# FFN up-projections: products of 512 columns into four banks, or of 256 columns into two

## The chip, the cores and the metric

The kernel runs on one core of a Trainium2 chip. The metric is device microseconds for one execution. TensorE is named PE in the profile, its weight loads PEld, VectorE DVE, ScalarE ACT, GpSimd POOL and SyncE SP.

## The reference

Two decoder layers over 256 positions of width 2048, all in float32. Layer 0 mixes with forgetting attention (16 heads of 128), layer 1 with sliding-window attention (32 query heads, 4 key heads of 64). After each mixer comes a gated ConvFFN. Every sub-layer is wrapped in a shift, a scale and a gate that come from a conditioning vector, and in a LayerNorm. The part that matters here:

```
def conv_ffn(h, w_up, conv_w, conv_b, w_down):          # D_FF = 5632, CONV_WIDTH = 3
    u = h @ w_up                                        # (256 x 2048) @ (2048 x 11264)
    up = jnp.pad(u, ((0, 0), (CONV_WIDTH - 1, 0), (0, 0)))
    u = sum(up[:, j:j + S] * conv_w[j] for j in range(CONV_WIDTH)) + conv_b
    g, val = u[..., :D_FF], u[..., D_FF:]
    return (jax.nn.silu(g) * val) @ w_down

x = layer_norm(DEEPNORM_ALPHA * x + (1.0 + gate) * F(x * (1.0 + scale) + shift), ln_g, ln_b)
```

## The kernel before

Every large product is made of three products in the float32r form. A weight tile `w` (two chunks of 128 rows by 512 columns, 512 KB, one DMA on SP's queue) is rounded by ACT into `wh` (L276), and DVE subtracts to get the remainder `wl` (L287). The activations are kept in the same way: `hHL[:, kc, 0, :]` is the rounded part `hH` of chunk kc (128 features by 256 positions), `hHL[:, kc, 1, :]`, right behind it in memory, the remainder `hL`. A product then adds `wh*hH + wh*hL + wl*hH`. A "tile" below is one such weight tile with all its products.

Three ways to use a tile stand side by side:

- `x_mm` (L298): activations are the stationary operand, weights move past in products of 512 columns. Their results are called `xs`. The down-projections of the FFN (`xs<-wh,gT`, `xs<-wl,gT`), both output projections and all of layer 1's input projections use it.
- `w_mm` (L325): weights are stationary, 128 columns at a time, and the activations move past in products of 256 columns: for each of the 8 cells (2 chunks, 4 column groups f) one product with `hH` and one with `hL`, both for the same weights, and then 8 products of `wl` with `hH`. Results are called `ws`, two banks of PSUM for the 4 column groups. Layer 0's query and key projections use it.
- the inner `use` of `w_stationary` (L344): the same, but `hH` and `hL` move past in one product of 512 columns, so that a bank holds `wh*hH` plus `wl*hH` in its left half and `wh*hL` in its right half. Results are called `wd`, four banks for the 4 column groups. The up-projections use it.

Each FFN has 22 column blocks of 512 for its two halves, gate and value, in two passes: 6 pairs of blocks (96 tiles) and the down-projection of what they give, then 5 pairs (80 tiles) and the rest of the down-projection. That is 352 tiles of up-projection in the two layers, and 176 of down-projection. When a block is done, a generator (`evac`, L1073) is put into a list and makes one step at each later tile: ACT copies the right half of a bank (L1060), DVE adds the left half to it (`summed`, L1061), ACT scales it by one tap of the convolution and adds the bias (L1066), DVE adds the other two taps (L1067, L1069), and then follows the SiLU (gate half) or the product with it and the split into `gT` (value half, L1089, L85, L86).

Beside this, the conditioning vectors of later sub-layers are computed on DVE (`acc`, L406) at a rate of so many steps a tile, and are finished on PE by small products (`sm<-acc,ones` and `sm<-ones,acc`). At the start of an FFN the activations come in over the first tiles: PE transposes the normalised x (`sm<-ident,x`), ACT and DVE turn that into `hHL`. `feed()` issues one such step within a tile.

Instructions are written in the order above and a scheduler then orders them by its own rules for each engine, except where `pin` holds them in program order. The semaphore waits follow from the tiles.

Of the kernel before, what the change touches and what calls it, by code (L numbers as in the profile page):

```python
# [10 lines left out]
F32 = mybir.dt.float32  # L11
F32R = mybir.dt.float32r
I32 = mybir.dt.int32
AF = mybir.ActivationFunctionType
ALU = mybir.AluOpType
AX = mybir.AxisListType

P = 128
D = 2048
S = 256  # L20
NT = S // P
KC = D // P
# [8 lines left out]
CW = 3  # L31
# [10 lines left out]
def hybrid_trunk(ctx: ExitStack, tc: tile.TileContext, a: dict, out: bass.AP):  # L42
    nc = tc.nc
# [9 lines left out]
    tp = ctx.enter_context(tc.tile_pool(name="tp", bufs=4))  # L53
# [3 lines left out]
    def wtile(name="w"):  # L57
        return wp.tile([P, 2, WB], F32, tag="w", name=name)

    def gtile(name="g"):  # L60
        return gp.tile([P, 2, S], F32R, tag="g", name=name)

    def ttile(name="t"):
        return tp.tile([P, 2 * S], F32, tag="t", name=name)

    def bank(name="sm"):
        return psp.tile([P, 512], F32, tag="ps", name=name)

    def w_banks():
        return [bank("ws").rearrange("p (a s) -> p a s", a=2) for _ in range(2)]  # L70
# [4 lines left out]
    def mm(o, lhsT, rhs, start=False, stop=False, **kw):  # L75
        return nc.tensor.matmul(o, lhsT, rhs, start=start, stop=stop, **kw)  # L76

    def pin(ins, on=True):

        if on:  # L80
            tc.keep_in_program_order(ins)

    def split(h, l, src):

        nc.scalar.copy(h, src)  # L85
        nc.vector.tensor_tensor(l, src, f32(h), op=ALU.subtract)  # L86
# [123 lines left out]
    def then(fn):  # L210

        work.append(fn)
        if len(work) == 1 and not ahead[0]:
            settle()
# [3 lines left out]
    def settle(left=0):  # L218
        while work and (ahead[0] > left or not left):
            f = work.pop(0)  # L220
            rest(f, *work)
            f()
# [24 lines left out]
    def defer(gen):  # L247

        post.append(gen)

    def run_post():
        for g in list(post):
            if next(g, post) is post:
                post.remove(g)
# [7 lines left out]
    def feed():  # L262

        if feeds and not fed[0]:
            fed[0] = True
            feeds.pop(0)()

    def stream(wsrc, row0, col, ks, use):

        for kc in ks[::2]:  # L270
            r0 = (row0 + kc) * P
            w = wtile()
            pin(nc.sync.dma_start(w, wsrc[r0:r0 + 2 * P, col:col + WB].rearrange("(k p) f -> p k f", p=P)), False)
            h = hl.tile([P, 2, WB], F32R, tag="wh", name="wh")
            l = hl.tile([P, 2, WB], F32R, tag="wl", name="wl")
            pin(nc.scalar.copy(h, w), False)  # L276

            def go(kc=kc, h=h, l=l):
                ahead[0] -= 1
                run_post()  # L280
                fed[0] = False
                use(kc, h, l)
                feed()
                tick()

            def residual_(w=w, h=h, l=l, go=go):
                pin(nc.vector.tensor_tensor(l, w, f32(h), op=ALU.subtract), go in behind)  # L287
                del residuals[go]

            if any(f in stops for f in work) and sum(f in behind for f in work) < 2:  # L290
                behind.add(go)
            ahead[0] += 1
            weights.add(go)
            residuals[go] = residual_
            work.append(go)
            settle(2)
# [28 lines left out]
    def w_mm(ps, kc, h, l, last=KC - 1, first=0):  # L325

        cells = [(i, f, ps[f // 2][:, f % 2, :]) for i in range(2) for f in range(4)]
        for i, f, o in cells:
            wh = h[:, i, f * P:(f + 1) * P]
            mm(o, wh, hH[:, kc + i, :], start=kc + i == first and f % 2 == 0, skip_group_check=True)  # L330
            mm(o, wh, hL[:, kc + i, :], skip_group_check=True)
        for i, f, o in cells:
            mm(o, l[:, i, f * P:(f + 1) * P], hH[:, kc + i, :], stop=kc + i == last, skip_group_check=True)

# [6 lines left out]

    def w_stationary(wsrc, col):

        ps = [bank("wd") for _ in range(4)]  # L344

        def use(kc, h, l):
            cells = [(i, f) for i in range(2) for f in range(4)]
            for i, f in cells:
                mm(ps[f], h[:, i, f * P:(f + 1) * P], hHL[:, kc + i].rearrange("p a s -> p (a s)"),
                   start=kc + i == 0)  # L350
            feed()
            for i, f in cells:
                mm(ps[f][:, :S], l[:, i, f * P:(f + 1) * P], hH[:, kc + i, :], stop=kc + i == KC - 1)

        stream(wsrc, 0, col, list(range(KC)), use)
        return ps


# [18 lines left out]
    def drain():  # L377
        while bg["wait"] or bg["run"]:
            step()

    def tick():
        ada_tick()
        if not feeds:
            step()
# [64 lines left out]
    def ada_need(l, v):  # L449
        n = 0  # L450
        while (l, v) not in cols and (l, v) not in gates:
            ada_step()
            n += 1
        if n:
            print("caught up", l, v, n)


    hHL = cst.tile([P, KC, 2, S], F32R, name="hHL")
    hH, hL = hHL[:, :, 0, :], hHL[:, :, 1, :]
# [593 lines left out]
    def conv_ffn(l):  # L1053
        w_up, w_dn = a["ffn_w_up"][l], a["ffn_w_down"][l]
        NB = DFF // WB
        cw = lambda j, f: ccol[:, l, j, f:f + 1]

        def summed(pf):
            s = tp.tile([P, S], F32, tag="s", bufs=2, name="s")
            nc.scalar.copy(s, pf[:, S:])  # L1060
            nc.vector.tensor_tensor(s, pf[:, :S], s, op=ALU.add)  # L1061
            return s

        def conv(s, f):
            u = tp.tile([P, S], F32, tag="u", bufs=2, name="u")
            nc.scalar.activation(u, s, AF.Identity, bias=cw(CW, f), scale=cw(2, f))  # L1066
            nc.vector.scalar_tensor_tensor(u[:, 1:], s[:, :S - 1], cw(1, f), u[:, 1:],  # L1067
                                           op0=ALU.mult, op1=ALU.add)
            nc.vector.scalar_tensor_tensor(u[:, 2:], s[:, :S - 2], cw(0, f), u[:, 2:],  # L1069
                                           op0=ALU.mult, op1=ALU.add)  # L1070
            return u

        def evac(ps, f0, then):  # L1073
            s = u = None
            for f in range(6):
                if u is not None:
                    then(f - 2, u)
                u = conv(s, f0 + f - 1) if s is not None else None
                s = summed(ps[f]) if f < 4 else None
                yield  # L1080

        def silu(sil):
            def f_(f, u):
                nc.scalar.activation(sil[f // 2][:, (f % 2) * S:(f % 2 + 1) * S], u, AF.Silu)
            return f_

        def gated(sil, gT):
            def f_(f, u):
                nc.vector.tensor_tensor(u, u, sil[f // 2][:, (f % 2) * S:(f % 2 + 1) * S], op=ALU.mult)  # L1089
                g = gtile("gT")  # L1090
                split(g[:, 0, :], g[:, 1, :], u)
                gT.append(g)
            return f_

        sbs = [(0, 6), (6, NB)]
        for si, (b0, b1) in enumerate(sbs):
            gT = []
            then(lambda: ada.update(rate=(0.52, 0.4)[l]))
            for b in range(b0, b1):
                ps = w_stationary(w_up, b * WB)  # L1100
                sil = [ttile("sil") for _ in range(2)]
                then(lambda ps=ps, b=b, sil=sil: defer(evac(ps, b * 4, silu(sil))))
                ps = w_stationary(w_up, DFF + b * WB)
                then(lambda ps=ps, b=b, sil=sil, gT=gT: defer(evac(ps, DFF // P + b * 4, gated(sil, gT))))

            def stat(kc, t, gT=gT):
                while kc >= len(gT):
                    run_post()
                return gT[kc][:, 0, t * P:(t + 1) * P], gT[kc][:, 1, t * P:(t + 1) * P]

            def ready(si=si):
                if si == 0:
                    drain()
                ada_need(l, 5)
                ada["rate"] = (0.8, 0.4)[l]

            then(ready)
            for d in range(D // WB):
                ps = x_stationary(w_dn, d * WB, b0 * 4, (b1 - b0) * 4, stat, (2, 4)[l] if si > 0 and d == D // WB - 1 else 0)
                then(lambda ps=ps, d=d, si=si: defer(residual(ps, d, gates[l, 5], si == len(sbs) - 1)))  # L1120
        then(lambda: (flush(), ada.update(gate_free=True)))
# [21 lines left out]
    for t in range(NT):  # L1143
        mu, rs, _ = moments[t]
# [31 lines left out]
```

## Time and profile before

| | us |
|---|---|
| median of 3 runs (2255.62 to 2256.58) | 2256.45 |
| the profiled execution: time | 2256.26 |
| the profiled execution: span from first to last instruction | 2254.5 |
| PE busy, weight loads busy | 2203.2, 1892.9 |
| DVE, ACT, POOL busy | 1852.2, 1193.7, 19.9 |

The span is 1.8 us shorter than the time of the same execution, and that execution is 0.2 us below the median, so a difference worked out in the span can be put on the median as it is. In a timeline, a row is a run of equal instructions: start, duration, engine, line, what is written from what, count. Products are pipelined: the last one of a run still drains while the next run has started, so how long a run holds PE is read from its start to the next row's start, not from its duration. The program's phases by time: layer 0's attention to 470 us, its FFN's first up-projections 472 to 747, down-projection to 881, second up-projections to 1107, down-projection to 1219; layer 1's attention to 1503; its FFN's first up-projections 1505 to 1780, down-projection to 1910, second up-projections to 2132, down-projection to the end.

### The profile page before, as it was taken

What the parts mean: (1) busy time and instruction counts of PE and PEld (TensorE: products, weight loads), DVE (VectorE), ACT (ScalarE), POOL (GpSimd) and SP (SyncE); (2) the same over time, 40 slices, a digit from 0 to 9 for tenths busy, and PEclk for the clock granted to TensorE, in tenths of its full rate; (3) what the DMA queues carried; (4) which work ended last, traced back from release to release, by engine and by line L of the source; (5) the groups of instructions that cost most, each with busy time, mean ns of one, the idle gap of its engine ahead of it and who ended that gap; (6) DMA issues with size and microseconds to landing.
All of it is one profiled execution on the core that took longest, in us unless ns stands there. A gap on an engine that the chain in (4) does not pass through costs nothing. (4 is left out here: it accounts for less than half of the span.)

```text
span 2254.5 us, 33348 instructions
## 1 busy us (share of the span) xinstructions
PE 2203.2 (98%) x12196; PEld 1892.9 (84%) x12196; DVE 1852.2 (82%) x2685; ACT 1193.7 (53%) x1873; POOL 19.9 (1%) x51
## 2 busy tenths in 40 slices
PE   7999999999999999999999999999999999999997
PEld 6988898788888888888887788888888888888886
DVE  7989998889988968978978989889988655676766
ACT  4546544356555433555534578646655533555542
POOL 0000000000000000000000000000000000000000
PEclk9999999999999999999999999999999999999999
DMA  9999999869978889878887867678887556666553
GB/s 345 393 372 311 341 379 355 305 222 307 313 243 273 316 292 333 287 226 285 280 307 261 288 202 262 219 254 290 285 268 242 187 194 190 190 192 189 189 194 111
DMA packets 287285, 602.68 MB, mean 267 GB/s; under 512 B 21830, under 2 KB 55304, under 8 KB 286608
## 3 DMA queue, kind: packets, MB, share of 16 engines
q1 hardware_dynamic: 286064, 595.86, 77.8%
q0 software_dynamic: 1056, 4.69, 0.6%
q8 instruction: 95, 1.56, 0.3%
q14 instruction: 70, 0.57, 0.1%
HBM read 598.37 MB, written 2.10 MB: 266 GB/s over the span
## 5 line engine op out<-in xcount | busy, mean ns | idle before, releaser
L276 ACT CAST wh<-w 128x1024 fp32r<-128x1024 f32 x728 | 764.7, 1051 | 802.0 <-PE wd L76 267.5
L287 DVE TENSOR_TENSOR wl<-w,wh 128x1024 fp32r<-128x1024 f32 x728 | 887.0, 1221 | 297.0 <-ACT wh L276 283.7
L76 PE MATMUL wd<-hHL,wh 128*128 128x512 f32 x2816 | 717.9, 397 | 1.1 <-DVE hHL L482 1.1
L76 PEld LDWEIGHTS wd<-hHL,wh 128*128 128x128 f32 x2816 | 503.4, 188 | 100.1 <-issue 2.9
L76 PEld LDWEIGHTS wd<-hHL,wl 128*128 128x128 f32 x2816 | 373.3, 188 | 32.8 <-DVE wl L287 1.6
L76 PE MATMUL wd<-hHL,wl 128*128 128x256 f32 x2816 | 379.6, 277 | 1.1 <-DVE wl L287 1.1
L406 DVE SCALAR_TENSOR_TENSOR acc<-wa,cact,acc 128x1024 f32<-128x1024 f32 x300 | 380.2, 1277 | 0.0
L76 PE MATMUL xs<-wh,gT 128*128 128x512 f32 x1408 | 349.7, 390 | 0.0
L76 PEld LDWEIGHTS xs<-wh,gT 128*128 128x128 f32 x1408 | 263.4, 188 | 54.2
L76 PE MATMUL xs<-wl,gT 128*128 128x512 f32 x704 | 189.3, 389 | 0.0
L76 PE MATMUL xs<-wh,hHL 128*128 128x512 f32 x704 | 185.5, 400 | 2.9 <-DVE hHL L86 2.7
L76 PEld LDWEIGHTS xs<-wl,gT 128*128 128x128 f32 x704 | 132.1, 188 | 27.6
L76 PEld LDWEIGHTS xs<-wh,hHL 128*128 128x128 f32 x704 | 128.9, 190 | 29.1 <-DVE hHL L86 3.5
L76 PE MATMUL ws<-hHL,wh 128*128 128x256 f32 x1024 | 133.2, 282 | 7.1 <-ACT wh L276 4.7
L1066 ACT ACTIVATE u<-s,ccol 128x256 f32<-128x256 f32 x176 | 104.6, 599 | 66.5 <-DVE s L1061 48.8
L76 PEld LDWEIGHTS ws<-hHL,wh 128*128 128x128 f32 x1024 | 125.1, 190 | 11.0 <-ACT wh L276 6.2
L76 PE MATMUL xs<-wh,oT 128*128 128x512 f32 x384 | 99.8, 398 | 0.1
L76 PE MATMUL xs<-wl,hHL 128*128 128x512 f32 x352 | 97.0, 395 | 1.5 <-DVE wl L287 1.5
L551 DVE SCALAR_TENSOR_TENSOR oacc<-wo,cact,oacc 128x512 f32<-128x512 f32 x111 | 79.5, 746 | 15.1 <-DMA wo<-in_ada_w_dram 10.0
L1067 DVE SCALAR_TENSOR_TENSOR u<-s,ccol,u 128x255 f32<-128x255 f32 x176 | 84.0, 479 | 5.6 <-ACT u L1066 5.6
L1069 DVE SCALAR_TENSOR_TENSOR u<-s,ccol,u 128x254 f32<-128x254 f32 x176 | 83.8, 477 | 1.1
L76 PEld LDWEIGHTS xs<-wh,oT 128*128 128x128 f32 x384 | 70.7, 190 | 14.3 <-ACT pT L719 0.5
(223 smaller groups left out, 1643.1 us busy)
## 6 DMA issues: line engine op xcount, KB each, us to landing
w<-in_ffn_w_up_dram SPq DMA_DIRECT2D x352, 512.0 KB, 4.6
wa<-in_ada_w_dram SPq DMA_DIRECT2D x320, 512.0 KB, 5.1
w<-in_ffn_w_down_dram SPq DMA_DIRECT2D x176, 512.0 KB, 4.2
w<-in_fox_w_in_dram SPq DMA_DIRECT2D x96, 512.0 KB, 6.6
wo<-in_ada_w_dram SPq DMA_DIRECT2D x128, 256.0 KB, 6.7
w<-in_swa_w_in_dram SPq DMA_DIRECT2D x40, 512.0 KB, 5.4
w<-in_fox_w_o_dram SPq DMA_DIRECT2D x32, 512.0 KB, 5.8
w<-in_swa_w_o_dram SPq DMA_DIRECT2D x32, 512.0 KB, 5.4
```

The costliest lines, as they stand in the source:

```text
L76: return nc.tensor.matmul(o, lhsT, rhs, start=start, stop=stop, **kw)
L276: pin(nc.scalar.copy(h, w), False)
L287: pin(nc.vector.tensor_tensor(l, w, f32(h), op=ALU.subtract), go in behind)
L406: pin(nc.vector.scalar_tensor_tensor(ac, wo, cact[:, k:k + 1], ac, op0=ALU.mult, op1=ALU.add), True)
L551: nc.vector.scalar_tensor_tensor(ac, wk, cact[:, kc:kc + 1], ac, op0=ALU.mult, op1=ALU.add)
L1066: nc.scalar.activation(u, s, AF.Identity, bias=cw(CW, f), scale=cw(2, f))
L1067: nc.vector.scalar_tensor_tensor(u[:, 1:], s[:, :S - 1], cw(1, f), u[:, 1:], op0=ALU.mult, op1=ALU.add)
L1069: nc.vector.scalar_tensor_tensor(u[:, 2:], s[:, :S - 2], cw(0, f), u[:, 2:], op0=ALU.mult, op1=ALU.add)
```

## The change

The up-projections use `w_mm` again: products of 256 columns for `wh` too, into two banks a block. `summed` goes; `conv` reads the bank itself, on ACT and on DVE, and `evac` has one step less. The two buffers of `s` become two more of `u`, so that the pool keeps its size and no operand's address moves. `w_mm` gets the `feed()` that `use` had. What it computes stays the same; the order in which terms are added changes a little.

```diff
@@ w_mm
             mm(o, wh, hH[:, kc + i, :], start=kc + i == first and f % 2 == 0, skip_group_check=True)
             mm(o, wh, hL[:, kc + i, :], skip_group_check=True)
+        feed()
         for i, f, o in cells:
@@ w_stationary
-        ps = [bank("wd") for _ in range(4)]
-
-        def use(kc, h, l):
-            cells = [(i, f) for i in range(2) for f in range(4)]
-            for i, f in cells:
-                mm(ps[f], h[:, i, f * P:(f + 1) * P], hHL[:, kc + i].rearrange("p a s -> p (a s)"),
-                   start=kc + i == 0)
-            feed()
-            for i, f in cells:
-                mm(ps[f][:, :S], l[:, i, f * P:(f + 1) * P], hH[:, kc + i, :], stop=kc + i == KC - 1)
-
-        stream(wsrc, 0, col, list(range(KC)), use)
+        ps = w_banks()
+        stream(wsrc, 0, col, list(range(KC)), lambda kc, h, l: w_mm(ps, kc, h, l))
@@ conv_ffn
-        def summed(pf):
-            s = tp.tile([P, S], F32, tag="s", bufs=2, name="s")
-            nc.scalar.copy(s, pf[:, S:])
-            nc.vector.tensor_tensor(s, pf[:, :S], s, op=ALU.add)
-            return s
-
-        def conv(s, f):
-            u = tp.tile([P, S], F32, tag="u", bufs=2, name="u")
-            nc.scalar.activation(u, s, AF.Identity, bias=cw(CW, f), scale=cw(2, f))
-            nc.vector.scalar_tensor_tensor(u[:, 1:], s[:, :S - 1], cw(1, f), u[:, 1:],
+        def conv(pf, f):
+            u = tp.tile([P, S], F32, tag="u", bufs=4, name="u")
+            nc.scalar.activation(u, pf, AF.Identity, bias=cw(CW, f), scale=cw(2, f))
+            nc.vector.scalar_tensor_tensor(u[:, 1:], pf[:, :S - 1], cw(1, f), u[:, 1:],
...
-            s = u = None
-            for f in range(6):
+            u = None
+            for f in range(5):
+                v = conv(ps[f // 2][:, f % 2, :], f0 + f) if f < 4 else None
                 if u is not None:
-                    then(f - 2, u)
-                u = conv(s, f0 + f - 1) if s is not None else None
-                s = summed(ps[f]) if f < 4 else None
+                    then(f - 1, u)
+                u = v
```

What this makes of PE's queue is seen where layer 0's activations have just come in, at about 490 us. `sm<-ident,x` are the transposes of x. Before, on PE:

```order
L76 MATMUL wd<-hHL,wh 128x512 x8
L469 MATMUL sm<-ident,x 128x128 x4
L76 MATMUL wd<-hHL,wl 128x256 x8
L76 MATMUL wd<-hHL,wh 128x512 x8
L76 MATMUL wd<-hHL,wl 128x256 x8
```

And now, on PE at the same place:

```order
L76 MATMUL ws<-hHL,wh 128x256 x16
L460 MATMUL sm<-ident,x 128x128 x4
L76 MATMUL ws<-hHL,wl 128x256 x8
L76 MATMUL ws<-hHL,wh 128x256 x16
L76 MATMUL ws<-hHL,wl 128x256 x8
```

Each group of 8 wide products has become 16 narrow ones; from there on nothing but such groups follows in PE's queue for 57 tiles, and the last transposes stand between a group of `wh` and one of `wl` as before. At the very start of the FFN (472 us) the scheduler has moved transposes forward, behind the products that warm PE up (`warm`). Before:

```order
L76 MATMUL warm<-ones 128x512 x4
L76 MATMUL wd<-hHL,wh 128x512 x8
L469 MATMUL sm<-ident,x 128x128 x4
L76 MATMUL wd<-hHL,wl 128x256 x8
L76 MATMUL wd<-hHL,wh 128x512 x3
```

And now:

```order
L76 MATMUL warm<-ones 128x512 x4
L76 MATMUL ws<-hHL,wh 128x256 x2
L460 MATMUL sm<-ident,x 128x128 x3
L76 MATMUL ws<-hHL,wh 128x256 x14
L460 MATMUL sm<-ident,x 128x128 x3
L76 MATMUL ws<-hHL,wl 128x256 x8
```

Three transposes now stand ahead of most of the first tile's products, and in layer 1 the order is the same. On DVE, where the first value block is evacuated (about 520 us), before:

```order
L287 TENSOR_TENSOR wl<-w,wh 128x1024
L1067 SCALAR_TENSOR_TENSOR u<-s,ccol,u 128x255
L1061 TENSOR_TENSOR s<-wd,s 128x256
L1069 SCALAR_TENSOR_TENSOR u<-s,ccol,u 128x254
L287 TENSOR_TENSOR wl<-w,wh 128x1024
L1089 TENSOR_TENSOR u<-u,sil 128x256
```

And now:

```order
L287 TENSOR_TENSOR wl<-w,wh 128x1024
L86 TENSOR_TENSOR gT<-u,gT 128x256
L1052 SCALAR_TENSOR_TENSOR u<-ws,ccol,u 128x255
L1074 TENSOR_TENSOR u<-u,sil 128x256
L1054 SCALAR_TENSOR_TENSOR u<-ws,ccol,u 128x254
L287 TENSOR_TENSOR wl<-w,wh 128x1024
```

The addition `s<-wd,s` is gone from between the splits of the weights (`wl<-w,wh`), and the taps read the bank `ws`.

More of the change, by code (lines that the diff above doesn't have):

```diff
@@ L1056, in conv_ffn @@
         cw = lambda j, f: ccol[:, l, j, f:f + 1]
-        def summed(pf):
-            s = tp.tile([P, S], F32, tag="s", bufs=2, name="s")
-            nc.scalar.copy(s, pf[:, S:])
-            nc.vector.tensor_tensor(s, pf[:, :S], s, op=ALU.add)
-            return s
-        def conv(s, f):
-            u = tp.tile([P, S], F32, tag="u", bufs=2, name="u")
-            nc.scalar.activation(u, s, AF.Identity, bias=cw(CW, f), scale=cw(2, f))
-            nc.vector.scalar_tensor_tensor(u[:, 1:], s[:, :S - 1], cw(1, f), u[:, 1:],
+        def conv(pf, f):
+            u = tp.tile([P, S], F32, tag="u", bufs=4, name="u")
+            nc.scalar.activation(u, pf, AF.Identity, bias=cw(CW, f), scale=cw(2, f))
+            nc.vector.scalar_tensor_tensor(u[:, 1:], pf[:, :S - 1], cw(1, f), u[:, 1:],
                                            op0=ALU.mult, op1=ALU.add)
-            nc.vector.scalar_tensor_tensor(u[:, 2:], s[:, :S - 2], cw(0, f), u[:, 2:],
+            nc.vector.scalar_tensor_tensor(u[:, 2:], pf[:, :S - 2], cw(0, f), u[:, 2:],
                                            op0=ALU.mult, op1=ALU.add)
```

## The prediction

> **What bounds the kernel now.** I read the page's busy shares first, then the busy time by stretches, then PE's waits in the up-projections, and last PE's timeline product by product.
>
> ```profile
> PE 2203.2 (98%) x12196; PEld 1892.9 (84%) x12196; DVE 1852.2 (82%) x2685; ACT 1193.7 (53%) x1873; POOL 19.9 (1%) x51
> ...
> w<-in_ffn_w_up_dram SPq DMA_DIRECT2D x352, 512.0 KB, 4.6
> ```
>
> The second row gives the count on which everything is multiplied: 352 tiles of up-projection. The stretches (columns: window, length, busy time and count of PE, PEld, DVE, ACT and POOL, granted clock, DMA share, GB/s):
>
> ```profile
> 472.00:503.00 31.00, 29.57 (x172) 25.12 (x173) 30.76 (x43) 17.88 (x26) 0.00 (x0) 1.00 0.74 248
> 503.00:652.00 149.00, 149.00 (x863) 129.86 (x862) 141.29 (x201) 88.56 (x137) 0.00 (x0) 1.00 0.89 304
> ```
>
> Once the activations are in, PE is busy in 149.00 of 149.00 us at full granted clock, although DVE stands at 95% and the DMA engines at 0.89. The waits from 503 to 747 us say the same; of PE's own these are all that are listed above 0.1 us:
>
> ```profile
> PEld wd L76 <- issue: 1.4, 6, 0.2
> ...
> PEld wd L76 <- ACT wh L276: 0.5, 2, 0.2
> ```
>
> So the up-projections cost what PE's products cost, one start after the other. What one tile costs is read from starts in PE's timeline, here layer 1's first stretch without any other work on PE, and from the window on it, whose third column counts weight loads:
>
> ```profile
> 1526.59 2.02 PE L76 MATMUL wd<-hHL,wh 128*128 128x512 f32 x8
> 1528.46 1.07 PE L76 MATMUL wd<-hHL,wl 128*128 128x256 f32 x8
> 1529.37 0.85 PE L76 MATMUL wd<-hHL,wh 128*128 128x512 f32 x3
> ...
> 1734.60 1.02 PE L76 MATMUL sm<-acc,ones 128*128 128x512 f32 x2
> ```
> ```profile
> 1526.60:1734.50 207.90, 207.90 (x1202) 181.06 (x1200) 15.41 (x38) 12.83 (x38) 1.00 0.84 276
> ```
>
> 1200 loads are 75 tiles of 16, so a tile takes (1734.60 - 1526.59) / 75 = 2.773 us: about 1.86 for its 8 wide products (0.233 each) and 0.91 for its 8 narrow ones (0.114 each).
>
> **What the same tile costs in products of 256 columns.** `w_mm` runs before too, in layer 0's query and key projections, on the same `hHL` and the same weight buffers. There are two speeds.
>
> ```profile
> 290.96 1.98 PE L76 MATMUL ws<-hHL,wh 128*128 128x256 f32 x16
> 292.78 1.07 PE L76 MATMUL ws<-hHL,wl 128*128 128x256 f32 x8
> ...
> 301.84 0.22 PE L76 MATMUL S<-Bm,A 128*128 128x128 f32 x1
> ...
> 302.76 2.05 PE L76 MATMUL ws<-hHL,wh 128*128 128x256 f32 x16
> 304.64 1.10 PE L76 MATMUL ws<-hHL,wl 128*128 128x256 f32 x8
> 305.59 0.22 PE L76 MATMUL S<-Bm,A 128*128 128x128 f32 x1
> ...
> 306.51 1.99 PE L76 MATMUL ws<-hHL,wh 128*128 128x256 f32 x16
> 308.34 1.07 PE L76 MATMUL ws<-hHL,wl 128*128 128x256 f32 x8
> 309.24 0.22 PE L76 MATMUL S<-Bm,A 128*128 128x128 f32 x1
> ```
>
> Four tiles in a row from 290.96 to 301.84 take 2.720 us each, 0.1133 a product: the quick pitch. The tile at 302.76 takes 2.83, 0.118 a product from its first to its last: the slow pitch. The tile at 306.51 settles within a few products and takes 2.73. Read at single products, every unbroken stretch of `ws` in this trace keeps its pitch from about its sixth product to its end, the quick one up to 120 products on. What stood on PE before it decides. So a quick tile saves 0.053 us against today's 2.773 and a slow one loses 0.057, and the whole change is a matter of which pitch each stretch falls into.
>
> At this point a rule speaks against the change. The Trainium skill (TensorE: Matmul & The Clock Gate, Back-to-back issue gap) gives an isolated warm product N/2.4 + 2.5 ns, so two halves would cost 2.5 ns more than one whole; by that estimate 2816 wide products split would add 7.0 us and give 2263.5. The trace here does not bear it out: 16 narrow products take 1.82 from 290.96, less than the 1.86 of the 8 wide ones.
>
> **The change part by part.** Its 352 tiles fall into stretches by what precedes them on PE; the counts are from the new order of PE's queue.
>
> Behind the down-projection, 36 tiles in layer 0 and 80 in layer 1, and behind the small products that end a conditioning vector (`sm<-ones,acc`), 44 in layer 0. No row shows narrow products behind `gT`, so I go by how wide ones start, and by narrow ones behind the same small products in layer 0's opening (`cps<-ones,oacc`):
>
> ```profile
> 1907.62 1.98 PE L76 MATMUL xs<-wh,gT 128*128 128x512 f32 x8
> 1909.43 1.07 PE L76 MATMUL xs<-wl,gT 128*128 128x512 f32 x4
> 1910.34 2.03 PE L76 MATMUL wd<-hHL,wh 128*128 128x512 f32 x8
> 1912.20 1.08 PE L76 MATMUL wd<-hHL,wl 128*128 128x256 f32 x8
> 1913.12 2.02 PE L76 MATMUL wd<-hHL,wh 128*128 128x512 f32 x8
> ```
> ```profile
> 981.97 2.11 PE L76 MATMUL wd<-hHL,wh 128*128 128x512 f32 x8
> 983.92 1.08 PE L76 MATMUL wd<-hHL,wl 128*128 128x256 f32 x8
> ```
> ```profile
> 80.06 1.62 PE L76 MATMUL cps<-ones,oacc 128*128 128x1 f32 x14
> 81.54 1.17 PE L76 MATMUL ws<-hHL,wl 128*128 128x256 f32 x8
> 82.55 0.62 PE L76 MATMUL xs<-wh,hHL 128*128 128x512 f32 x2
> ```
>
> The down-projection itself runs at 1.81 us for 8 wide products, twice the quick pitch, and the tile behind it reads like the one behind the small products (first narrow group 1.08 in both); narrow products behind `cps` settle (8 in 1.01 with the step at their start, as in the row at 1525.58 below). I take the quick pitch for all 160: 160 x 0.053 = -8.5. Bounds: -8.5 and 160 x 0.057 = +9.1.
>
> Behind the wide products that end a gate vector (`sm<-acc,ones`, at 1734.60), 33 and 15 tiles. Nothing like it precedes `ws` in the trace, and most entries seen in it end in the quick pitch (8 of 13 in the next paragraph, both kinds of the last), so quick: 48 x 0.053 = -2.5, bounds -2.5 and +2.7.
>
> Behind the last transposes of the entering activations, 57 tiles in layer 0 and 75 in layer 1.
>
> ```profile
> 492.44 0.60 PE L469 MATMUL sm<-ident,x 128*128 128x128 f32 x4
> 492.80 1.19 PE L76 MATMUL wd<-hHL,wl 128*128 128x256 f32 x8
> 493.83 2.03 PE L76 MATMUL wd<-hHL,wh 128*128 128x512 f32 x8
> ...
> 1525.58 1.18 PE L76 MATMUL wd<-hHL,wl 128*128 128x256 f32 x8
> ```
>
> Today wide products follow and end either pitch; now it would last. The row at 492.80 is one that stays slow (1.03 to the next start), that at 1525.58 one that settles (1.01, to 1526.59). Of 13 such groups behind transposes of x, the first at 39 us and the last at 1525.58, 8 settle and 5 do not. That is close to even, so I take one of the two stretches for quick and one for slow: 57 quick and 75 slow is -3.0 + 4.3, the reverse -4.0 + 3.2, in the middle +0.3. Bounds: both quick -7.0, both slow +7.5.
>
> The 12 tiles in which activations still enter: PE waits there today (1.43 us in 472 to 503). Transposes now stand ahead of 14 of the first 16 products, so a late x is waited for earlier; the work behind it is the same. I take 0; bounds 0 and twice today's wait in both layers, +2.9.
>
> The evacuation:
>
> ```profile
> L1061 DVE TENSOR_TENSOR s<-wd,s 128x256 f32<-128x256 f32 x176 | 70.9, 417 | 0.0
> L1060 ACT COPY s<-wd 128x256 f32<-128x256 f32 x176 | 59.6, 364 | 2.1 <-DVE u L1069 1.5
> ```
>
> Removed: 70.9 us of DVE and 59.6 of ACT. PE's 149.00 of 149.00 hides it, so 0 on the path; were the cover gone, DVE would have 0.2 us a tile in hand (4 x 0.417 over 8 tiles), more than the 0.053 by which a tile gets shorter. The taps read PSUM instead of `s`, and `s<-wd,s` itself reads PSUM in 417 ns, so they are not dearer. A block holds its two banks until the last tap of its five steps, about five tiles; two blocks hold four of eight banks, so the next block does not wait. Next in line, were PE quicker, are the DMA engines:
>
> ```profile
> 288.20:301.70 13.50, 13.47 (x119) 1.00 1.02 381
> ```
>
> Here the quick pitch held with the DMA engines at 1.02, so 0.89 rising by 2% takes nothing back.
>
> The sum: -8.5 - 2.5 + 0.3 = -10.7, so 2256.45 - 10.7 = 2245.8 (the profiled execution of 2256.26 is within 0.2 of the median).
>
> **The rivals.**
>
> Both long stretches settle: -8.5 - 2.5 - 7.0 = -18.0, 2238.4. For it speak the majority of 8 of 13 and that the three groups of layer 0's opening, behind narrow products as now, all settle.
>
> Both stay slow: -8.5 - 2.5 + 7.5 = -3.5, 2252.9, no change that shows (a measurement of this kernel tells about 0.2%, 4.5 us, from none). For it speaks the row at 492.80, which stands where the new stretches begin, and that both layers now have one order.
>
> The slower one: the narrow products fall into the slow pitch behind the down-projection too. Place: the entry at 1910.34 and its like in layer 0, 116 tiles. Price: 116 x 0.110 = 12.8, 2258.6. It decides from 164 slow tiles of 340 on (0.053 against 0.057). Against it: the down-projection's 1.81 is already in step with the quick pitch. For it: the wide products behind it run at 1.86 at once.
>
> The loss sits in reading `hHL` beside the weights and not in the width: then 16 narrow products take the 1.86 of the 8 wide ones and a start more each, at most the 0.01 by which 1.82 exceeds 1.81, and the time is 2256.45 + 352 x 0.01 = 2260. The page named above would have it so, from a fixed cost. Against it are the rows from 290.96, with the same operand.
>
> The quick pitch is there but something else bounds: DVE at 95% in the first pass of layer 0, or weights landing later. 2256. Against it: the removed 70.9 us, and the row at 1.02.
>
> **How the numbers follow.** One long stretch quick and one slow 0.35; both quick 0.25; both slow 0.17; slow behind the down-projection 0.11; loss in the operand 0.05; another bound 0.04; waits at the entry or at banks 0.03. Faster: the first two and a little of the fourth with everything else quick, 0.62. Same 0.19: both slow, another bound, less what noise moves over. Slower 0.19: the rest. The range reaches from both quick with a rounding of 2 us to the operand's case and a little beyond, 2236 to 2261; the forecast's own is 2242 to 2250.
>
> **What would show it.** In the new trace starts of narrow products 113 ns apart, and a tile of 2.72, wherever `ws` follows `gT` or a small product; a pitch that is fixed by the last transposes in each layer's first pass and then stands for 57 and 75 tiles; PE still at full busy time; DVE less busy by about 70 us, ACT by about 60. I am wrong if the pitch changes within an unbroken stretch, if it is slow behind the down-projection, or if PE shows waits for `wl`, `wh` or a bank between tiles.

## The result, and the profile after

The changed kernel takes 2274.46 us (median of 4 runs, 2269.14 to 2278.11), the kernel before 2256.22 beside it: ratio 1.0079, 95% interval [1.0059, 1.01]. It is 0.8% slower. The forecast was 2245.8, the range 2236 to 2261. The profiled execution after took 2274.03 us, its span is 2272.3.

The page's busy shares, then the stretches of the first table of the prediction (same columns), and the waits of the weight loads from 503 to 747 us:

```profile
PE 2220.5 (98%) x15012; PEld 2037.8 (90%) x15012; DVE 1800.5 (79%) x2509; ACT 1138.2 (50%) x1697; POOL 21.5 (1%) x51
```
```profile
472.00:503.00 31.00, 29.02 (x244) 28.27 (x243) 30.61 (x42) 17.78 (x25) 0.00 (x0) 1.00 0.78 254
503.00:652.00 149.00, 149.00 (x1267) 149.00 (x1266) 132.12 (x172) 78.43 (x108) 0.00 (x0) 1.00 0.90 301
```
```profile
PEld ws L76 <- ACT wh L276: 1.0, 4, 0.2
PEld ws L76 <- issue: 1.0, 4, 0.2
```

PE is still busy in 149.00 of 149.00 us at full granted clock, ACT and DVE have more air than before, and nothing new is waited for. So no wait took the place of another: PE's products themselves became dearer. PE's timeline shows it at all four kinds of entry (start, duration, engine, line, what, count):

```profile
492.21 1.19 PE L76 MATMUL ws<-hHL,wl 128*128 128x256 f32 x8
493.24 2.05 PE L76 MATMUL ws<-hHL,wh 128*128 128x256 f32 x16
495.12 1.10 PE L76 MATMUL ws<-hHL,wl 128*128 128x256 f32 x8
496.07 2.05 PE L76 MATMUL ws<-hHL,wh 128*128 128x256 f32 x16
...
1004.02 0.95 PE L76 MATMUL sm<-ones,acc 128*128 128x1 f32 x8
1004.83 2.13 PE L76 MATMUL ws<-hHL,wh 128*128 128x256 f32 x16
1006.80 1.11 PE L76 MATMUL ws<-hHL,wl 128*128 128x256 f32 x8
1007.74 2.05 PE L76 MATMUL ws<-hHL,wh 128*128 128x256 f32 x16
1009.63 1.11 PE L76 MATMUL ws<-hHL,wl 128*128 128x256 f32 x8
...
1534.92 2.05 PE L76 MATMUL ws<-hHL,wh 128*128 128x256 f32 x16
...
1746.92 1.02 PE L76 MATMUL sm<-acc,ones 128*128 128x512 f32 x2
...
1922.44 1.07 PE L76 MATMUL xs<-wl,gT 128*128 128x512 f32 x4
1923.34 2.05 PE L76 MATMUL ws<-hHL,wh 128*128 128x256 f32 x16
1925.23 1.10 PE L76 MATMUL ws<-hHL,wl 128*128 128x256 f32 x8
1926.17 2.05 PE L76 MATMUL ws<-hHL,wh 128*128 128x256 f32 x16
...
2149.48 1.75 PE L76 MATMUL xs<-wh,gT 128*128 128x512 f32 x7
```

Behind the last transposes (492.21), behind the small products (1004.83), behind the down-projection (1923.34) and, not shown, behind `sm<-acc,ones`: everywhere the slow pitch. 75 tiles from 1534.92 to 1746.92 take 2.827 us each (before 2.773), the last 80 from 1923.34 to 2149.48 the same. From start rows like these, the four phases of up-projection as a whole (each layer's first one with the last `warm` products ahead of it):

| phase (us) | layer 0 first | layer 0 second | layer 1 first | layer 1 second | sum |
|---|---|---|---|---|---|
| before | 276.17 | 225.79 | 276.27 | 221.88 | 1000.11 |
| changed | 281.28 | 229.70 | 281.28 | 226.13 | 1018.39 |

The phases lose 18.3 us, the span 17.8: the whole loss is here, nearly all of it 0.053 us in each of some 340 tiles.

### The profile page after: what moved, and what is told of

Read it like the earlier page. It is cut to its first block, busy times and chain, and to the rows that moved or that the text cites. A ratio compares the mean times of both kernels' runs of the same rounds, so it can differ in the third digit from the quotient of the medians.

```text
span 2272.3 us, 38505 instructions
## 1 busy us (share of the span) xinstructions
PE 2220.5 (98%) x15012; PEld 2037.8 (90%) x15012; DVE 1800.5 (79%) x2509; ACT 1138.2 (50%) x1697; POOL 21.5 (1%) x51
## 5 line engine op out<-in xcount | busy, mean ns | idle before, releaser
L76 PE MATMUL ws<-hHL,wh 128*128 128x256 f32 x6656 | 858.8, 282 | 9.5 <-ACT wh L276 5.1
L76 PEld LDWEIGHTS ws<-hHL,wh 128*128 128x128 f32 x6656 | 814.6, 189 | 18.5 <-ACT wh L276 8.6
L76 PE MATMUL ws<-hHL,wl 128*128 128x256 f32 x3328 | 460.4, 281 | 1.9 <-DVE wl L287 1.9
L76 PEld LDWEIGHTS ws<-hHL,wl 128*128 128x128 f32 x3328 | 420.9, 189 | 2.5 <-DVE wl L287 2.4
L1051 ACT ACTIVATE u<-ws,ccol 128x256 f32<-128x256 f32 x176 | 97.9, 560 | 16.8 <-DVE u L1054 16.8
L1054 DVE SCALAR_TENSOR_TENSOR u<-ws,ccol,u 128x254 f32<-128x254 f32 x176 | 83.4, 477 | 2.1
L1052 DVE SCALAR_TENSOR_TENSOR u<-ws,ccol,u 128x255 f32<-128x255 f32 x176 | 82.8, 477 | 0.7 <-ACT u L1051 0.6
L76 PEld LDWEIGHTS xs<-wl,hHL 128*128 128x128 f32 x352 | 65.8, 189 | 16.7 <-DVE wl L287 2.8
L612 DVE TENSOR_TENSOR t<-xs,gate 128x512 f32<-128x512 f32 x48 | 32.8, 687 | 33.5 <-PE xs L76 33.3
```

The lines of the kernel that those rows point to most:

```text
L612: pin(nc.vector.tensor_tensor(tmp, ps[t], gate[:, c0:c0 + 512], op=ALU.mult), end)
L1051: nc.scalar.activation(u, pf, AF.Identity, bias=cw(CW, f), scale=cw(2, f))
L1052: nc.vector.scalar_tensor_tensor(u[:, 1:], pf[:, :S - 1], cw(1, f), u[:, 1:], op0=ALU.mult, op1=ALU.add)
L1054: nc.vector.scalar_tensor_tensor(u[:, 2:], pf[:, :S - 2], cw(0, f), u[:, 2:], op0=ALU.mult, op1=ALU.add)
```

## The experiments

Theory after the result: `ws` has a quick pitch (113.3 ns a product) and a slow one (117.8), and what stands on PE ahead of a stretch picks one, but picks the slow one nearly always. Rivals: the shorter evacuation is to blame, or the place of `hHL` in memory.

**The evacuation by itself.** `narrow_old_evac` has narrow products, but the four banks and the addition of halves of before:

```diff
-mm(ps[f], h[:, i, f * P:(f + 1) * P], hHL[:, kc + i].rearrange("p a s -> p (a s)"),
-   start=kc + i == 0)
+wh = h[:, i, f * P:(f + 1) * P]
+mm(ps[f][:, :S], wh, hH[:, kc + i, :], start=kc + i == 0, skip_group_check=True)
+mm(ps[f][:, S:], wh, hL[:, kc + i, :], skip_group_check=True)
...
```

> Narrow products as in the changed kernel, but four banks a block, wh*hL into the right half, and the old evacuation with its copy and addition: the product width alone is changed. Three theories. Entry: narrow products on hHL have a quick (113 ns) and a slow (118 ns) pitch, what stands ahead of a stretch picks one, and the evacuation plays no part; then this runs at the slow pitch like the changed kernel, 2274 us (2266 to 2279). Evacuation: the slow pitch comes from the taps' reading of the two banks that PE fills; then this is quick, 352 tiles x 0.053 us below the kernel before, 2238. Alignment: the slow pitch, and the wide products' 233 ns too, come from where hHL begins (64 bytes past a multiple of 128); then 2274 as by the first.

Measured: 2262.87 us, ratio 1.0026 [1.0017, 1.0036]. No theory had this: it lies between the 2238 of the evacuation and the 2274 (2266 to 2279) of the entry.

`wide_short_evac` has the wide products of before, but evacuates as the changed kernel does, from the left half of each bank; what `wh*hL` gave is left out of the sum. Against the changed kernel's line:

```diff
-v = conv(ps[f // 2][:, f % 2, :], f0 + f) if f < 4 else None
+v = conv(ps[f][:, :S], f0 + f) if f < 4 else None
```

> The kernel before, wide products into four banks, but evacuated as in the changed kernel: the taps read a bank's left half and the copy and addition go. It leaves out the part wh*hL, which lies in the right half. Entry and relative address: the evacuation is hidden behind PE, 2256, within 0.2%. Evacuation: if reading the banks with the taps is what slows PE, 2274; if the 70.9 us of DVE were on the path, up to 70 less.

Measured: 2255.46 us, ratio 1.0 [0.9991, 1.001]. The shorter evacuation is worth nothing beside wide products, as the prediction had it. That narrow products with the old evacuation are quicker than with the new one is a matter of pitch, seen in layer 1's first pass of `narrow_old_evac`:

```profile
1533.16 1.17 PE L76 MATMUL wd<-hHL,wl 128*128 128x256 f32 x8
1534.16 1.98 PE L76 MATMUL wd<-hHL,wh 128*128 128x256 f32 x16
1535.98 1.07 PE L76 MATMUL wd<-hHL,wl 128*128 128x256 f32 x8
1536.88 1.98 PE L76 MATMUL wd<-hHL,wh 128*128 128x256 f32 x16
```

Behind the same transposes as at 1534.92 above, the tile takes 2.72: this stretch of 75 tiles settled (phase 272.71 us), and so did 39 tiles of layer 0's second pass. Layer 0's first pass (281.19) and both stretches behind the down-projection stayed slow. So both pitches occur with the old evacuation, and it is not what sets them; that it changes which stretches settle is not excluded.

**Something ahead of each block.** `narrow_reset` puts two wide products, into a bank that nobody reads, ahead of each of the 44 blocks of the changed kernel:

```diff
...
+if kc == 0:
+    o = bank("turn")
+    for f in range(2):
+        mm(o, h[:, 0, f * P:(f + 1) * P], hHL[:, 0].rearrange("p a s -> p (a s)"), start=True, stop=True)
 w_mm(ps, kc, h, l)
```

> The changed kernel with two wide products (512 columns, into a bank that nobody reads) ahead of the first tile of each of the 44 blocks: 88 products of 0.233 us, 20.5 us of PE added. Entry: if a stretch takes its pitch from what stands ahead of it, and wide products lead into the quick one as they did in the kernel before, 2256 - 18 + 20.5 = 2258, with every block at 113 ns; if two are too few to turn it, 2274 + 20.5 = 2295. Evacuation: 2295, since the taps read the banks as before. Alignment: 2295 with blocks at 118 ns, or 2258; it does not say.

Measured: 2263.99 us, ratio 1.0035 [1.0022, 1.0048], with some 20 us of added products in it. Two places in its timeline:

```profile
681.74 0.62 PE L76 MATMUL turn<-hHL,wh 128*128 128x512 f32 x2
682.20 2.05 PE L76 MATMUL ws<-hHL,wh 128*128 128x256 f32 x16
684.08 1.11 PE L76 MATMUL ws<-hHL,wl 128*128 128x256 f32 x8
...
885.33 0.63 PE L76 MATMUL turn<-hHL,wh 128*128 128x512 f32 x2
885.79 1.99 PE L76 MATMUL ws<-hHL,wh 128*128 128x256 f32 x16
887.62 1.07 PE L76 MATMUL ws<-hHL,wl 128*128 128x256 f32 x8
```

At 885.79, behind the down-projection, the tile is quick (1.83 and 0.90 to the next start), where the changed kernel's is slow: the entry does decide. At 682.20, within a slow stretch, the same two products changed nothing. Of 38 blocks with 100 or more products in one piece behind their turn, 34 ran quick, but in 31 of these the products ahead of the turn were quick already. Where they were not, the block became quick at 500.09 (slow products ahead), 885.79 and 1917.58 (the down-projection ahead), and stayed slow at 682.20, 705.27, 728.34 and 1763.91.

**Few turns, at the long stretches.** `narrow_turns` is the changed kernel with 8 wide products ahead of the second block of each first pass, 8 more in layer 0 behind the conditioning products, and 2 ahead of each second pass; the new last argument of `w_stationary` is their number, issued as in `narrow_reset`:

```diff
-ps = w_stationary(w_up, b * WB)
+ps = w_stationary(w_up, b * WB, 2 if si == 1 and b == b0 else 0)
...
-ps = w_stationary(w_up, DFF + b * WB)
+ps = w_stationary(w_up, DFF + b * WB, 8 if si == 0 and (b == 0 or (l == 0 and b == 4)) else 0)
```

> The changed kernel with a few wide products (512 columns of hHL, into a bank that nobody reads) put in front of stretches of narrow ones: 8 ahead of the second block of each layer's first pass (behind the last transposes), 8 more in layer 0 where the products that end a conditioning vector have passed, 2 ahead of the second pass's first block in both layers. They cost PE 3 x 8 x 0.233 + 2 x 2 x 0.233 = 6.5 us. If what stood on PE before a stretch sets its pitch, and wide products ahead of it turn most of the stretches quick (312 tiles at 2.720, 40 at 2.826, against 2.773 of before): 2256.2 - 312 x 0.053 + 40 x 0.053 + 6.5 = 2248, faster than both. If a turn only takes for some stretches, between 2255 and 2270. If the pitch does not hang on the entry and the reset kernel's quick stretches came from the wide products' presence every block: 2274.5 + 6.5 = 2281.

Measured: 2250.9 us (11 runs), ratio 0.998 [0.9971, 0.9989], against 2255.69 of the kernel before: quicker than both.

```profile
497.20 1.10 PE L76 MATMUL ws<-hHL,wl 128*128 128x256 f32 x8
498.14 2.03 PE L76 MATMUL turn<-hHL,wh 128*128 128x512 f32 x8
500.01 1.98 PE L76 MATMUL ws<-hHL,wh 128*128 128x256 f32 x16
501.83 1.07 PE L76 MATMUL ws<-hHL,wl 128*128 128x256 f32 x8
...
677.55 1.11 PE L76 MATMUL ws<-hHL,wl 128*128 128x256 f32 x8
678.50 2.02 PE L76 MATMUL turn<-hHL,wh 128*128 128x512 f32 x8
680.36 2.05 PE L76 MATMUL ws<-hHL,wh 128*128 128x256 f32 x16
```

The turn at 498.14 has slow tiles directly ahead of it and made the 55 behind it quick (2.72 from there on); those at the other three long stretches made 73, 36 and 80 quick. The 39 tiles behind the small products of layer 0's second pass ran quick without a turn of their own. The turn at 678.50 failed, and its 24 tiles stayed slow: 24 x 0.107 = 2.6 us, most of the 2.9 by which the measured time lies above the expected 2248. Its phases: 279.15, 221.70, 275.36, 218.08, sum 994.29, 5.8 less than before with the added products in it. All five long pieces in which a turn failed, here and in `narrow_reset`, lie behind `sm<-acc,ones`; one short piece of 24 products behind it (656.65 in `narrow_reset`) did become quick.

**The place of `hHL`.** It starts at byte 25280 of a partition, 192 past a multiple of 256; all weight buffers start at multiples of 512. These kernels only move it, by spare bytes ahead of it (`narrow_...` from the changed kernel, `wide_...` from the one before):

```diff
+cst.tile([P, 16], F32, name="lead")
 hHL = cst.tile([P, KC, 2, S], F32R, name="hHL")
 hH, hL = hHL[:, :, 0, :], hHL[:, :, 1, :]
-cst.tile([P, 24], F32, name="gap")
+cst.tile([P, 8], F32, name="gap")
```

That is `narrow_aligned` and `wide_aligned` (25344). `narrow_512` and `wide_512` have it at 25600, `narrow_plus32` at 25312, `narrow_plus96` and `wide_plus96` at 25376; what lies behind stays, or moves by 512 bytes.

> The changed kernel with hHL moved up by 64 bytes to a multiple of 128, and the gap behind it shortened by as much, so that no other operand moves. Alignment: the slow pitch goes, all stretches at 113 ns, 2274 - 352 x 0.107 = 2237 us. Entry: the pitch does not depend on the address, 2274 (2266 to 2279). Evacuation: 2274.

> The kernel before with hHL moved up by 64 bytes to a multiple of 128 and nothing else moved. Alignment: its 2816 wide products go from 233 ns to the 226.7 of the down-projection, whose moving operand lies on a multiple of 512 bytes: 2256 - 2816 x 0.0066 = 2237.5 us. Entry and evacuation: no change, 2256.

> The changed kernel with hHL moved from 25280 to 25600, a multiple of 512 as the weight buffers are, and all behind it moved by 512 bytes, so that only hHL's place against the 512s is new. Offsets of 192 bytes (two pitches, 113 and 118) and of 256 (one, 120) are known. Relative address: the pitch hangs on where the moving operand lies against the weights; in the down-projection both begin on multiples of 512 and it always runs at 226.7 ns for 512 columns, so here only 113.3 should be left: 2256 - 352 x 0.053 = 2237 us, whatever stands ahead. Entry: two pitches as before, the slow one behind the same entries, 2274 (2262 to 2279). Any other offset than 192 fixes a slow pitch: 2295 as at 256.

> The kernel before with the same move of hHL to a multiple of 512. Relative address: wide products at 226.7 instead of 233, 2256 - 2816 x 0.0066 = 2237.5 us. Entry: 2256. Any other offset than 192 is slower: 2263 as at 256.

> The changed kernel with hHL moved up by 32 bytes only (offset 224 against the 512s, 96 against 128), nothing else moved. Relative address: a pitch of its own between those at 192 and 256 or a set of two, the same in all stretches behind like entries; 2237 to 2300, which tells how fine the dependence is. Entry: as at 192, 2274 (2262 to 2279).

> The changed kernel with hHL 96 bytes further on (25376, 32 bytes past a multiple of 128), nothing else moved. If the place of hHL against 128 bytes sets the pitch, this is a fourth place: a single pitch in all stretches, as at 0 and 96, near the 118.3 ns of 96 (mirror image): about 2281. If only the distance to a multiple of 64 counts (32 and 96 alike): 118.3 again, 2282.8. If it is 64 bytes that are special and everything else is 120: 2296.

> The kernel before (wide products) with hHL 96 bytes further on (25376, 32 past a multiple of 128), nothing else moved. At 64 past, wide products take 0.233 and wl's narrow ones 0.1133; at 0 past, 0.227 to 0.233 and 0.120 (2263). If the place against 128 bytes sets the pitch of each form: narrow ones at about 0.118, +352 x 8 x 0.005 = +14 us, less what the wide ones gain (0 to 0.006 x 2816 = 17): 2253 to 2270. If wide products don't care for the place: 2270.

The first tiles behind the down-projection in `narrow_aligned`, and then in `wide_aligned`:

```profile
1940.99 2.08 PE L76 MATMUL ws<-hHL,wh 128*128 128x256 f32 x16
1942.90 1.12 PE L76 MATMUL ws<-hHL,wl 128*128 128x256 f32 x8
1943.86 2.08 PE L76 MATMUL ws<-hHL,wh 128*128 128x256 f32 x16
```
```profile
1916.24 1.98 PE L76 MATMUL wd<-hHL,wh 128*128 128x512 f32 x8
1918.06 1.11 PE L76 MATMUL wd<-hHL,wl 128*128 128x256 f32 x8
1919.01 2.00 PE L76 MATMUL wd<-hHL,wh 128*128 128x512 f32 x8
1920.85 1.12 PE L76 MATMUL wd<-hHL,wl 128*128 128x256 f32 x8
```

At a multiple of 256 narrow products take 120 ns (2.87 for 24), whatever precedes them, in every stretch: 2295.62 us, ratio 1.0174 [1.0159, 1.0189]. In `wide_aligned` the wide ones take 0.227 in the first tile, at 1916.24, but 0.230 from the next tile on (1.84 for 8 from 1919.01), instead of 0.233, and the narrow ones of `wl` 0.119 instead of 0.114. A tile takes 2.793 instead of 2.773, and the kernel with wide products loses too: 2263.17, 1.0032 [1.002, 1.0043]. At 25600 it is the same: 2296.2, 1.0181 [1.0165, 1.0196], and 2263.69, 1.0038 [1.0023, 1.0053]. At 25312 the narrow pitch is 118.3 on average, in steps from 115 to 123: 2282.82, 1.0125 [1.0108, 1.0142]. At 25376 it is 116.7: 2267.81, 1.0054 [1.004, 1.0068], with wide products 2267.26, 1.0051 [1.0038, 1.0065] (0.233 and 0.117, 2.807 a tile). Most of these times were not expected: alignment and relative address had 2237 to 2237.5 at multiples of 128 and 512, the entry theory 2274 and 2256 there and 2274 at 25312, and the three guesses for `narrow_plus96` began at 2281. The multiples of 256, which alignment had among the best places, are the slowest of all for narrow products; only the rival that any other offset than 192 is slower was right at 25600.

**Which length counts.** `narrow_64` (25664), `narrow_448` (25536), `narrow_320` (25408), `narrow_160` (25504) and `narrow_128` (25472) are the changed kernel with `hHL` moved and what lies behind it 512 bytes further; in `narrow_behind512` only what lies behind moves, in `narrow_all512` both do.

> The changed kernel with hHL 384 bytes further on (25664: again 64 bytes past a multiple of 128, but 64 past a multiple of 512 where the changed kernel has it 192 past), what lies behind it moved by 512 bytes. If the place against 128 bytes sets the pitch: again two pitches, 113.3 and 117.8, and a time between 2238 and 2278, with no stretch at 120. If another distance counts (512 bytes, or hHL's own old place): another pitch, 118 to 120 in every stretch, 2280 to 2296.

> The changed kernel with hHL where it was (25280, 192 past a multiple of 512) and all that lies behind it moved by 512 bytes. If hHL's place against 512 bytes decides: two pitches again (113.3 and 117.8), some quick stretches in layer 0's attention as before, 2238 to 2278. If the moved buffers made narrow_64 slow in every stretch: 117.8 everywhere, 2276.7.

> The changed kernel with hHL and all behind it moved by 512 bytes (hHL at 25792, again 192 past a multiple of 512). If only places against 512 bytes count: as the changed kernel, two pitches, 2238 to 2278, and quick stretches in layer 0's attention. If the absolute place counts: one pitch, 117 to 120, 2268 to 2296.

> The changed kernel with hHL at 25536 (448 past a multiple of 512, 64 past one of 128, 192 past one of 256), what lies behind moved by 512 bytes. If the place against 256 bytes decides: as at 192, two pitches, 2238 to 2278. If that against 512 does: another pitch, 113 to 120 in every stretch, 2238 to 2296.

> The changed kernel with hHL at 25408 (320 past a multiple of 512, 64 past one of 128 and of 256), what lies behind moved by 512 bytes. If the place against 256 bytes decides: as narrow_64 (64 past 512), 117.8 in every stretch, 2276.7. If that against 512 does: any single pitch, or two.

> The changed kernel with hHL at 25504 (160 past a multiple of 256, 32 past one of 128), what lies behind moved by 512 bytes. If 128 bytes count: as 32 past, 116.7 in every stretch, 2267.8. If 256 count, the place is its own: between its neighbours' 113.3 and 120, 2238 to 2296; one quick pitch would give 2238, faster than both.

> The changed kernel with hHL at 25472 (a multiple of 128, 128 past a multiple of 256), what lies behind moved by 512 bytes. If 128 bytes count: 120.0 in every stretch, 2296. If 256 count: another pitch than 120, 2238 to 2285.

The stretch of layer 0's attention that was quick at 290.96 before, in `narrow_64` and in `narrow_448`:

```profile
291.56 2.05 PE L76 MATMUL ws<-hHL,wh 128*128 128x256 f32 x16
293.45 1.10 PE L76 MATMUL ws<-hHL,wl 128*128 128x256 f32 x8
294.39 2.04 PE L76 MATMUL ws<-hHL,wh 128*128 128x256 f32 x16
```
```profile
288.00 1.99 PE L76 MATMUL ws<-hHL,wh 128*128 128x256 f32 x16
289.83 1.07 PE L76 MATMUL ws<-hHL,wl 128*128 128x256 f32 x8
290.74 1.98 PE L76 MATMUL ws<-hHL,wh 128*128 128x256 f32 x16
```

All places together, by the bytes past a multiple of 256 (pitch of narrow products in unbroken stretches, from starts in PE's timeline):

| past 256 | kernels | pitch, ns | time, us | ratio, interval |
|---|---|---|---|---|
| 0 | narrow_aligned, narrow_512 | 120.0 | 2295.62, 2296.2 | above |
| 32 | narrow_plus96 | 116.7 | 2267.81 | above |
| 64 | narrow_64, narrow_320 | 117.8 | 2276.67, 2277.98 | 1.0094 [1.008, 1.0108], 1.0095 [1.008, 1.011] |
| 128 | narrow_128 | 118.7 or 120.0 | 2289.07 | 1.0149 [1.0132, 1.0166] |
| 160 | narrow_160 | 117.4 or 118.7 | 2280.86 | 1.0113 [1.0098, 1.0128] |
| 192 | changed kernel | 113.3 or 117.8 | 2274.46 | 1.0079 [1.0059, 1.01] |
| 192 | narrow_behind512 | 113.3 or 117.8 | 2273.56 | 1.0074 [1.0057, 1.0092] |
| 192 | narrow_all512 | 113.3 or 117.8 | 2271.97 | 1.007 [1.0049, 1.0091] |
| 192 | narrow_448 | 113.3 or 117.8 | 2268.96 | 1.0053 [1.0037, 1.007] |
| 224 | narrow_plus32 | 118.3 | 2282.82 | above |

Places 256 bytes apart behave alike (64 and 320, 192 and 448, the two multiples of 256), places 128 apart do not (32 and 160, 64 and 192). So the theory of 128 bytes, which had expected two pitches in `narrow_64`, 116.7 in `narrow_160` and 120.0 in every stretch of `narrow_128`, fell, and 256 stands for the places tried. Of the seven, the old one alone has the pitch of 113.3, and there the entry picks (at 128 and 160 a stretch also has one of two pitches, 1.3 ns apart). Even there the phases hardly ever got it without help: in the five profiled runs at 192 without added products, all 10 stretches behind the down-projection were slow, all 10 long ones behind `sm<-acc,ones` began slow, and 3 of 10 behind the last transposes and 1 of 5 behind `sm<-ones,acc` were quick. Which ones settle differs between these kernels, and the runs of one kernel scatter by up to 10 us at 192, by up to 2.8 at 64. The counts are from one profiled execution of each kernel.

## Why the prediction was wrong, point by point

**What bounds.** Right: PE's products, one start after the other; evacuation, DMA engines, banks and `wl`/`wh` played no part. The rows of `s<-wd,s` are gone, and total busy time fell by 51.7 us on DVE and 55.5 on ACT (the prediction had about 70 and 60), without effect; `wide_short_evac` shows the same for the edit alone.

**Two pitches, and what precedes picks.** Right in kind and in size: 2.72 and 2.827 a tile, and the same stretch behind the down-projection is slow in the changed kernel and quick behind two added products. Within unbroken stretches the pitch held, over 1920 products. The one stretch that changed had a stall in it (`narrow_old_evac` at 1761 us: slow for 7 products, then two starts 0.15 and 0.10 us late, quick from there).

**The step that failed: "I take the quick pitch for all 160".** The term was -8.5; measured, these tiles take 2.827, and 160 x 0.053 is +8.5, near the upper bound of +9.1. The reasoning from the down-projection's own pace ("in step with the quick pitch") was wrong: narrow products behind it start at 118 ns at once and stay there. The rival "slow behind the down-projection too" named this place and a price for it, but gave it 0.11.

**The two other entry terms failed with it.** Behind `sm<-acc,ones`: -2.5 forecast, 48 x 0.053 = +2.5 measured. Behind the last transposes: +0.3 forecast, 132 x 0.053 = +7.0 measured, the upper bound nearly. The count "8 settle and 5 do not" came from short groups in other surroundings; 3 of 10 is what these entries gave. The three terms sum to +18.0; what the phases lost beyond that is 0.3 us, waits at entry included, so the 0 for these was about right, and outside the phases 0.5 came back. 2256.2 + 18.3 - 0.5 is 2274.0, within the runs. Of the rivals, the one with both long stretches slow was right on its place, but kept the other terms quick. The bounds of the terms together (+19.3) held it; the range, which ended at the operand's case, did not, since the entries were taken as nearly independent, and all went one way.

**What the prediction overlooked** stood in its own rows. In the kernel before, `wl`'s narrow products run quick in each tile (0.91 for 8), and 8 wide products stand ahead of them each time. The prediction says of the transposes that wide products "end either pitch", but does not ask which pitch they lead into; the change took away just these. `narrow_reset` and `narrow_turns` put a few back, and most of the narrow products became quick. That wide products turn a slow pitch is shown where the products ahead were not quick already (500.09, 885.79, 1917.58 and four of the five turns in `narrow_turns`), and it does not hold everywhere (682.20 and 680.36 above).

**The rival of the operand** ("the loss sits in reading `hHL`") was named at 0.05 with a cost per start. The place of `hHL` does set which pitches there are, from 113.3 to 120.0, not by a cost per start: two narrow products cost 0.227 at the quick pitch, less than the wide one's 0.233, and 0.236 at the slow one. The Trainium skill (TensorE: Matmul & The Clock Gate, Back-to-back issue gap) gives an isolated warm product one fixed cost, from which the estimate of 2263.5 was worked out; no run here shows a single fixed cost.

**Still open:** why the pitch hangs on 256 bytes, whether on the distance to the weights' buffers or on `hHL`'s own address (the weights were never moved against 256 bytes), and why some turns take and others do not.

## What to carry to other kernels

Where PE runs without a gap, time one product by starts, in the stretch where it will run and behind the same predecessor: a form that is quick in short groups can be slow for 80 tiles on end. When entries share a mechanism, add their bounds with one sign and put that sum into the range. And try a few places for the moving operand within 256 bytes: with the same instructions this one took from 2268 to 2296 us by the place alone.

## What the hardware showed that was not expected

The pitch of float32r products depends on where the moving operand starts: 256 columns take 113.3 to 120.0 ns, and in the up-projections with wide products 512 columns take 230.1 (0 past 256), 232.7 (192 past) or 233.4 ns (32 past) on average. Of these three places the first is the best for the wide products and the worst for the narrow ones, so a kernel that mixes them has to weigh both.

Each product brings its own weight load, also where two products in a row use the same weights. Groups of weight loads in the changed kernel, and before it:

```profile
L76 PEld LDWEIGHTS ws<-hHL,wh 128*128 128x128 f32 x6656 | 814.6, 189 | 18.5 <-ACT wh L276 8.6 <-DVE hHL L86 4.3 <-ACT hHL L85 2.0
```
```profile
L76 PEld LDWEIGHTS wd<-hHL,wh 128*128 128x128 f32 x2816 | 503.4, 188 | 100.1 <-issue 2.9 <-ACT hHL L478 1.9 <-ACT wh L276 1.0
```

6656 loads are one for each narrow product of `wh` (5632 of the up-projections and 1024 of layer 0's attention); with wide products there were 2816 and 1024. A load lasts 188 to 189 ns, longer than a narrow product's pitch, so loads overlap each other and leave no idle time (PEld 149.00 of 149.00, before 129.86). The quick pitch has the same: from 1540 to 1720 us PEld is busy in 180.00 of 180.00 us in `narrow_turns`, where the stretch is quick, and in the changed kernel, where it is slow. So the busy loads alone don't tell the two pitches apart; whether they have a part in them was not tried.
